# A decoder step on one core: its opening with zero products first, another order of loads, other banks, and squares summed on TensorE

## The chip, the cores and the metric

The kernel runs on one core of one Trainium2 chip. The core has five engines, each with its own instruction stream in a fixed order: TensorE (PE in the profile, its weight loads PEld), VectorE (DVE), ScalarE (ACT), GpSimd (POOL) and SyncE (SP), which here issues all loads and stores. They work on SBUF; TensorE writes into PSUM, eight banks of 128 x 512 fp32, which DVE and ACT read. The metric is device microseconds (us) of one execution. The time before is the median of three runs.

## What is computed

One layer of a hybrid decoder for 512 prompt tokens and 8 x 8 sample tokens, 576 columns in all, of width 1024. The part that the change touches is the first norm and the first columns of the big input product:

```python
def rmsnorm(x, g):
    xf = x.astype(jnp.float32)
    y = xf * lax.rsqrt(jnp.mean(xf * xf, -1, keepdims=True) + EPS)
    return (y * g.astype(jnp.float32)).astype(x.dtype)
...
    h = rmsnorm(x, lp['norm1_g'])
    z = h @ lp['w_in']
...
    qk, mconv_new = causal_dwconv(mconv, z[..., M_QK:M_V], lp['m_conv_w'], lp['m_conv_b'])
...
    li = (z[..., M_I:M_F] + lp['m_i_bias']).astype(f32)
    lf = jax.nn.log_sigmoid((z[..., M_F:M_END] + lp['m_f_bias']).astype(f32))
...
    zr = z[..., R_START:R_END]
    prev = jnp.concatenate([rshift[:, None].astype(zr.dtype), zr[:, :-1]], axis=1)
    xm = zr + (prev - zr) * lp['r_mix']
```

After it come the mLSTM heads, the RWKV-7 recurrence, two gated branches, w_out, a second norm with a convolutional feed-forward part, a third norm with a gate, and the final norm.

## The kernel before

Activations lie with channels on the partitions: x is eight tiles of 128 channels (k = 0 to 7) by 576 tokens, and nearly all work is done in two halves of 288 tokens (`HF`, `half(hf)`). A tile j of `w_in` has 128 output columns; its weights come as two pieces of 128 x 512, one for k 0 to 3 and one for k 4 to 7.

Every wide product is done in three fp32r products: a value is split into a high part (a rounding copy on ACT) and a low part (value less high part, on DVE), and high x high, high x low and low x high are added in one PSUM bank (`half_k`, L190 to L193). So a tile half takes 3 x 8 = 24 products of 128 x 288. `wsplit` (L154, L155) and `wload` (L169, L170) split weights; in the opening the high parts are nh and the low parts nl. `raw_split` (L417, L418) multiplies x by the norm's gain and splits it into xrh and xrl.

The opening (L376 to L463) starts before the norm is known. Three tiles, `lead` = 12, 13, 0, are multiplied with x times gain only, and the norm's factor is applied when they are copied out (`evac_pad` with rs, L355, reading `rsr` in SBUF; without rs it is an ACT copy, L352). The other tiles use `xs1`, the normed and split x (`norm_half`, L268 to L270), as do the 128 columns with the gate rows ("if", L458: the 8 real columns padded to 64, high parts in 64 and low parts in 64, two products for each k).

The norm's factor of a half comes from `add_squares` (ACT squares, L253; for the opening POOL multiplies and adds into acc, L247 and L254), then `rms_half`: three products of acc with a column of ones give the sums by token (L234), DVE scales (L235), POOL takes the power -0.5 (L216), ACT widens to 128 x 384 (L238) and three transposes on TensorE spread it over the partitions (L241). The result is copied to rsr.

PSUM banks have tags: three "d", two "r", one each of "s", "c" and "m". A bank is used again only when its readers are done. Before, tile 12 has two of "d", tile 13 "s" and "c", tile 0 both "r". The gate rows then take the third "d" and an "r", tile 4 two of "d", and tile 8, which comes later by `dense` (L174), "d" banks again.

SP issues the loads in the order in which they are written, apart from waits for buffers: x0 w00 x1 x2 w01 x3 to x7 (first halves; w00 is piece 0 of the first lead tile), cst (identity, ones and masks), w10 w11, the second halves of x, vec, w20 w21. Raw weight pieces have six buffers.

The order of each engine's instructions is set by a planner when the program is built: it runs the program against its own estimate of times, and gives each engine, among the instructions that are ready, the one written first. On the chip that order is fixed. At the very start four products of zeros run on TensorE from a tile `warm` (L394), which DVE clears and into which ACT copies one column; that copy is ACT's first instruction and makes it load its function table.

Of the kernel before, what the change touches and what calls it, by code (L numbers as in the profile page):

```python
# [15 lines left out]
P = 128  # L16
# [79 lines left out]
def build(tc, nc, I, O):  # L96
# [12 lines left out]
    with st0:  # L109
# [119 lines left out]
        def rms_half(pl, acc, hf, pt="m"):  # L229

            pm = bank(pt)
            cols = pl.tile([P, 3], F32, tag="rsc", name="rsc", bufs=2)
            for w, o in enumerate(HB):
                TE.matmul(pm[:, w:w + 1], acc[:, hf * HF + o:hf * HF + o + P], ones[:, 0:1], start=True, stop=True)  # L234
# [4 lines left out]
            b = bank(pt)  # L239
# [136 lines left out]
        with ExitStack() as stn:  # L376
# [14 lines left out]
            S.copy(warm[:, 0:1], nhalf)  # L391
# [4 lines left out]
            xdma(0, 0)  # L396
            wdma(0, 0)
            xdma(1, 0)
            xdma(2, 0)
            wdma(0, 1)  # L400
            for k in range(3, KD):
                xdma(k, 0)
            SY.dma_start(cst, I["cst"])
            wdma(1, 0)
            wdma(1, 1)
# [3 lines left out]
            wdma(2, 0)  # L409
            wdma(2, 1)  # L410
# [3 lines left out]
            lws = [wsplit(raw[0], KD, npool, ("nh", "nl"), 6)]  # L414
            def raw_split(k, hf):
# [5 lines left out]
            xr = []  # L421
            for k in range(KD):
                xr.append(raw_split(k, 0))
                add_squares(npool, acc, xt[k], k, 0, G)
            S.copy(rsr[:, half(0)], rms_half(npool, acc, 0, "m"))
            lws.append(wsplit(raw[1], KD, npool, ("nh", "nl"), 6))
            for k in range(KD):
                add_squares(npool, acc, xt[k], k, 1, G)
            S.copy(rsr[:, half(1)], rms_half(npool, acc, 1, "m"))
            lws.append(wsplit(raw[2], KD, npool, ("nh", "nl"), 6))  # L430
            for k in range(KD):
                for i, j in enumerate(lead):
                    half_k(lps[j][0], lws[i], xr[k], k, KD, slice(0, HF))
            for k in range(KD):
                xr.append(raw_split(k, 1))
            norm_half(npool, xt, rsr[:, half(0)], 0, "norm1_g", xs1)
            for i, j in enumerate(lead):
                for k in range(KD):
                    half_k(lps[j][1], lws[i], xr[KD + k], k, KD, slice(0, HF))

# [7 lines left out]
            w4 = wload(I["w_in"][4], KD)  # L448
            lps["if"] = [bank("d", "pd")]
            lps[4] = [bank("d", "pd")]  # L450
            lps["if"].append(bank("r", "pd"))
            lps[4].append(bank("d", "pd"))
            for hf in range(2):
                if hf:
                    norm_half(npool, xt, rsr[:, half(1)], 1, "norm1_g", xs1)
# [1064 lines left out]
```

## Time and profile before

| what | value |
|---|---|
| median of 3 runs | 1078.46 us (1074.89 to 1079.7) |
| the profiled execution | 1070.66 us |
| its span | 1068.8 us |
| mean granted TensorE clock | 0.996 |
| TensorE busy | 1045.1 us, 98% |
| DVE, ACT, POOL busy | 73%, 48%, 24% |
| moved by DMA | 114.74 MB, mean 107 GB/s |

The profile is of one execution; the time beside the span is what lies around it. A row of the time line has the start, the time, the engine, the line of the code, the operation, output <- inputs, and in brackets how long the engine had stood idle and what released it. A row by groups has the count (x8), the busy time and mean ns behind the bar, and then the idle time in front of the group. fp32 products appear as two records each.

### The profile page before, as it was taken

To read this page: it belongs to the slowest core of one execution; us is meant where nothing else is said; L and a number is where in the kernel's file an instruction comes from. 1 tells how busy PE (TensorE), PEld (TensorE's weight loads), DVE (VectorE), ACT (ScalarE), POOL (GpSimd) and SP (SyncE) were. 2 spreads that over 40 slices of the span, in tenths; PEclk is the share of its full clock that TensorE was granted. 3 is DMA by queue.
4 is the path that set the end of the run, shared out by engine and by line. 5 is a ranking of instruction groups with operands and counts; after the bars stand their busy time and mean duration, and the time that the engine had idled before them with its cause. 6 is when DMAs were issued, how large, how long until landed. Compare 5 with 4: busy or idle time off the path is not lost.

```text
span 1068.8 us, 23108 instructions
## 1 busy us (share of the span) xinstructions
PE 1045.1 (98%) x8991; PEld 1009.0 (94%) x8991; DVE 777.0 (73%) x1645; ACT 508.8 (48%) x1072; POOL 254.5 (24%) x394
## 2 busy tenths in 40 slices
PE   8899999999999999999999999999999999999996
PEld 7899999999989988999999999999999999999996
DVE  7887657876786676356775799945998569975864
ACT  7684634462553344334343465522565236553822
POOL 7622112221131021001401253200343005410300
PEclk9999999999999999999999999999999999999999
DMA  7243412442342322446850312322233322342513
GB/s 252 95 127 93 108 53 58 103 141 60 88 143 75 81 84 91 143 151 234 263 181 1 116 37 93 110 90 75 85 99 97 102 70 90 94 117 67 165 40 123
DMA packets 90894, 114.74 MB, mean 107 GB/s; under 512 B 35617, under 2 KB 45217, under 8 KB 90785
## 3 DMA queue, kind: packets, MB, share of 16 engines
q1 hardware_dynamic: 90784, 113.27, 34.7%
q8 instruction: 70, 1.15, 0.4%
q14 instruction: 40, 0.32, 0.1%
HBM read 94.79 MB, written 18.45 MB: 106 GB/s over the span
## 4 chain that ended last, share of the span: by engine, by line
PE 90%; DVE 4%; DMA 4%; ACT 1%; issue 1%; SPq 0%; POOLq 0%; DVEq 0%; ACTq 0%
PE pd L193 55%; PE pd L306 20%; PE pm L655 1%; PE pm L1106 1%; PE pm L1136 1%; PE pm L835 1%; PE pm L809 1%; DMA yin<-d_y 1%; PE pm L910 1%; DVE xnf L268 1%; PE pm L917 1%; PE pm L1199 1%; PE pm L775 0%; DMA d_y<-og 0%; DMA wr<-i_w_out 0%
## 5 line engine op out<-in xcount | busy, mean ns | idle before, releaser
L169 ACT CAST wh<-wr 128x512 fp32r<-128x512 f32 (+2 forms) x170 | 101.7, 599 | 173.4 <-PE pd L193 140.7
L170 DVE TENSOR_TENSOR wl<-wr,wh 128x512 fp32r<-128x512 f32 (+2 forms) x170 | 118.8, 702 | 82.4 <-ACT wh L169 80.8
L193 PE MATMUL pd<-actl,wh 128*128 128x288 f32 x384 | 111.9, 295 | 0.0
L193 PE MATMUL pd<-acth,wl 128*128 128x288 f32 x384 | 111.4, 295 | 0.0
L193 PE MATMUL pd<-acth,wh 128*128 128x288 f32 x384 | 110.3, 295 | 0.0
L193 PEld LDWEIGHTS pd<-actl,wh 128*128 128x128 f32 x384 | 71.8, 188 | 0.0
L193 PEld LDWEIGHTS pd<-acth,wl 128*128 128x128 f32 x384 | 71.6, 188 | 0.0
L193 PEld LDWEIGHTS pd<-acth,wh 128*128 128x128 f32 x384 | 71.1, 188 | 0.1
L294 ACT CAST wh<-ws 128x512 fp32r<-128x512 f32 x76 | 47.1, 619 | 48.9 <-PE pd L306 24.8
L295 DVE TENSOR_TENSOR wl<-ws,wh 128x512 fp32r<-128x512 f32 x76 | 58.1, 765 | 8.4 <-ACT wh L294 7.9
L300 POOL TENSOR_TENSOR ws<-wr 128x512 f32<-128x512 f32 x19 | 31.7, 1670 | 96.9 <-DVE wl L295 54.1
L294 ACT CAST wh<-wr 128x512 fp32r<-128x512 f32 x57 | 35.3, 619 | 38.5 <-PE pd L306 24.0
L1333 POOL COPY o_f<-u 128x2 f32<-128x2 f32 x22 | 26.6, 1209 | 110.8 <-DVE u L1330 109.2
L295 DVE TENSOR_TENSOR wl<-wr,wh 128x512 fp32r<-128x512 f32 x57 | 39.5, 693 | 7.3 <-ACT wh L294 7.2
L216 POOL TENSOR_TENSOR rsc<-rsc,nhalf 128x3 f32<-128x3 f32 x8 | 9.3, 1167 | 131.1 <-DVE rsc L235 131.1
L1342 DVE SCALAR_TENSOR_TENSOR y<-u,vec,y 128x592 f32<-128x592 f32 x44 | 38.5, 875 | 1.2 <-ACT y L1340 1.0
L253 ACT ACTIVATE sq<-res 128x288 f32<-128x288 f32 x40 | 17.7, 445 | 36.0 <-DVE res L1279 18.5
L193 PE MATMUL pd<-mgh,ol 128*128 128x288 f32 x112 | 33.0, 296 | 0.0
L193 PE MATMUL pd<-mgl,oh 128*128 128x288 f32 x112 | 33.0, 295 | 0.0
L193 PE MATMUL pd<-mgh,oh 128*128 128x288 f32 x112 | 32.8, 295 | 0.0
L1370 DVE TENSOR_TENSOR res<-res,pd 128x288 f32<-128x288 f32 x48 | 20.9, 450 | 15.7 <-PE pd L193 15.5
L193 PE MATMUL pd<-xa0h,wh 128*128 128x288 f32 x86 | 26.4, 307 | 3.0 <-ACT zr L352 1.6
(825 smaller groups left out, 3949.4 us busy)
## 6 DMA issues: line engine op xcount, KB each, us to landing
wr<-i_w_in SPq DMA_DIRECT2D x92, 256.0 KB
wr<-i_f_up SPq DMA_DIRECT2D x88, 256.0 KB
wr<-i_f_down SPq DMA_DIRECT2D x32, 256.0 KB
d_th<-gst SPq DMA_DIRECT2D x16, 288.0 KB
th<-d_th SPq DMA_DIRECT2D x16, 288.0 KB
wr<-i_w_br SPq DMA_DIRECT2D x16, 256.0 KB
wr<-i_w_out SPq DMA_DIRECT2D x16, 256.0 KB
wr<-i_ple_gate SPq DMA_DIRECT2D x16, 256.0 KB
```

The source lines that it names most:

```text
L169: S.copy(wh[:, 0:nk, :], wr[:, 0:nk, :])
L170: V.tensor_tensor(wl[:, 0:nk, :], wr[:, 0:nk, :], wh[:, 0:nk, :], ALU.subtract)
L193: TE.matmul(pm[:, 0:HF], w[:, k % 4, :], a[:, c], start=k == 0 and i == 0, stop=k == n - 1 and i == 2)
L253: S.activation(sq, x[:, c], AF.Square)
L268: V.scalar_tensor_tensor(xn, xt[k][:, c], vcol(gname, k), rs, ALU.mult, ALU.mult)
L294: S.copy(wh, w)
L295: V.tensor_tensor(wl, w, wh, ALU.subtract)
L300: e.tensor_tensor(t, a, b, ALU.add)
L306: TE.matmul(pm[:, 0:HF], w[a][:, k, :], xs[k][b], start=not more and k == 0 and i == 0, stop=k == 3 and i == 2, skip_group_check=more)
L1333: G.tensor_copy(o_f[:, j, 0:2], u[:, TP:TP + 2])
L1342: V.scalar_tensor_tensor(y, u[:, i:i + 592], w(i), y, ALU.mult, ALU.add)
L1370: V.tensor_tensor(x1[m][:, c], x1[m][:, c], pss[hf][:, 0:HF], ALU.add)
```

## The change

It works in the opening alone.

- ACT's first copy goes to a tile of its own (warm1), so the zero products need only DVE's clearing. POOL sets a column of ones (one), which does not come from cst.
- The loads: x0 w00 x1 x2 x3 w01 x4 x5 w10 x6 x7 w11 w20 w21, then cst, the second halves of x, vec.
- All of half 0's `raw_split` stands first, then the splits of the second and third lead tile.
- Half 0's squares: ACT squares all eight x tiles (sq0, four buffers), and TensorE multiplies each with the ones, three products for each k, added up over k in three columns (288 to 290) of one bank "m". POOL adds nothing for half 0. The spread of half 0 is transposed into the same bank, and the norm of half 0 reads it there; the copy to rsr comes behind it.
- Half 1 keeps squares on ACT and additions on POOL; its three sums go into a bank "d", written behind the second lead tile's half 1, its spread into "m".
- Tile 8's products join tile 4's in the opening, in both "r" banks; the gate rows go to "s" and "c".

```diff
-        def rms_half(pl, acc, hf, pt="m"):
-
-            pm = bank(pt)
+        def rms_half(pl, acc, hf, pt="m", sums=None):
+
+            b = sums if acc is None else bank(pt)
+            pm = (sums if sums is not None else b)[:, HF:HF + 3]
             cols = pl.tile([P, 3], F32, tag="rsc", name="rsc", bufs=2)
-            for w, o in enumerate(HB):
-                TE.matmul(pm[:, w:w + 1], acc[:, hf * HF + o:hf * HF + o + P], ones[:, 0:1], start=True, stop=True)
+            if acc is not None:
+                for w, o in enumerate(HB):
+                    TE.matmul(pm[:, w:w + 1], acc[:, hf * HF + o:hf * HF + o + P], ones[:, 0:1], start=True, stop=True)
             V.tensor_scalar(cols, pm[:, 0:3], 1.0 / D, EPS, ALU.mult, ALU.add)
...
-            b = bank(pt)
...
-            S.copy(warm[:, 0:1], nhalf)
+            S.copy(npool.tile([P, 1], F32, name="warm1"), nhalf)
+            one = npool.tile([P, 1], F32, name="one")
+            G.memset(one, 1.0)
...
-            xdma(0, 0)
-            wdma(0, 0)
-            xdma(1, 0)
-            xdma(2, 0)
-            wdma(0, 1)
-            for k in range(3, KD):
-                xdma(k, 0)
+            for what in "x0 w00 x1 x2 x3 w01 x4 x5 w10 x6 x7 w11 w20 w21".split():
...
             SY.dma_start(cst, I["cst"])
-            wdma(1, 0)
-            wdma(1, 1)
             for k in range(KD):
                 xdma(k, 1)
             SY.dma_start(vec[:, KD:NV], I["vec"][:, KD:NV])
-            wdma(2, 0)
-            wdma(2, 1)
...
-            xr = []
+            xr = [raw_split(k, 0) for k in range(KD)]
+            lws.append(wsplit(raw[1], KD, npool, ("nh", "nl"), 6))
+            lws.append(wsplit(raw[2], KD, npool, ("nh", "nl"), 6))
+
+            sums = bank("m")
+            sqs = []
             for k in range(KD):
-                xr.append(raw_split(k, 0))
-                add_squares(npool, acc, xt[k], k, 0, G)
-            S.copy(rsr[:, half(0)], rms_half(npool, acc, 0, "m"))
-            lws.append(wsplit(raw[1], KD, npool, ("nh", "nl"), 6))
+                sqs.append(npool.tile([P, HF], F32, tag="sq0", name="sq0", bufs=4))
+                S.activation(sqs[k], xt[k][:, half(0)], AF.Square)
+                for i, j in enumerate(lead):
+                    half_k(lps[j][0], lws[i], xr[k], k, KD, slice(0, HF))
+                for w, o in enumerate(HB):
+                    TE.matmul(sums[:, HF + w:HF + w + 1], sqs[k][:, o:o + P], one, start=k == 0 and w == 0, stop=k == KD - 1, skip_group_check=True)
+            rs0 = rms_half(npool, None, 0, sums=sums)
+            for k in range(KD):
+                xr.append(raw_split(k, 1))
+            norm_half(npool, xt, rs0, 0, "norm1_g", xs1)
+            S.copy(rsr[:, half(0)], rs0)
             for k in range(KD):
                 add_squares(npool, acc, xt[k], k, 1, G)
-            S.copy(rsr[:, half(1)], rms_half(npool, acc, 1, "m"))
-            lws.append(wsplit(raw[2], KD, npool, ("nh", "nl"), 6))
-            for k in range(KD):
-                for i, j in enumerate(lead):
-                    half_k(lps[j][0], lws[i], xr[k], k, KD, slice(0, HF))
-            for k in range(KD):
-                xr.append(raw_split(k, 1))
-            norm_half(npool, xt, rsr[:, half(0)], 0, "norm1_g", xs1)
             for i, j in enumerate(lead):
                 for k in range(KD):
                     half_k(lps[j][1], lws[i], xr[KD + k], k, KD, slice(0, HF))
+                if i == 1:
+                    rs1 = rms_half(npool, acc, 1, "m", bank("d"))
...
-            w4 = wload(I["w_in"][4], KD)
-            lps["if"] = [bank("d", "pd")]
-            lps[4] = [bank("d", "pd")]
-            lps["if"].append(bank("r", "pd"))
-            lps[4].append(bank("d", "pd"))
+            more = [4, 8]
+            wm = [wload(I["w_in"][j], KD) for j in more]
+            lps["if"] = [bank("s", "pd"), bank("c", "pd")]
+            lps[4] = [bank("d", "pd") for _ in range(2)]
+            lps[8] = [bank("r", "pd") for _ in range(2)]
             for hf in range(2):
                 if hf:
-                    norm_half(npool, xt, rsr[:, half(1)], 1, "norm1_g", xs1)
+                    norm_half(npool, xt, rs1, 1, "norm1_g", xs1)
+                    S.copy(rsr[:, half(1)], rs1)
...
                     if hf:
-                        dense_half(lps[4][hf], w4, xs1, hf, (k,))
+                        for j, w in zip(more, wm):
+                            dense_half(lps[j][hf], w, xs1, hf, (k,))
                 if not hf:
-                    dense_half(lps[4][hf], w4, xs1, hf)
+                    for j, w in zip(more, wm):
+                        dense_half(lps[j][hf], w, xs1, hf)
```

More of the change, by code (lines that the diff above doesn't have):

```diff
@@ L395, in build @@
             SY.dma_start(vec[:, 0:KD], I["vec"][:, 0:KD])
-            xdma(0, 0)
-            wdma(0, 0)
-            xdma(1, 0)
-            xdma(2, 0)
-            wdma(0, 1)
-            for k in range(3, KD):
-                xdma(k, 0)
+            for what in "x0 w00 x1 x2 x3 w01 x4 x5 w10 x6 x7 w11 w20 w21".split():
+                if what[0] == "x":
+                    xdma(int(what[1]), 0)
+                else:
+                    wdma(int(what[1]), int(what[2]))
             SY.dma_start(cst, I["cst"])
-            wdma(1, 0)
-            wdma(1, 1)
             for k in range(KD):
```

## The prediction

> **What bounds the kernel now.** I read the page first: the busy shares, then the chain that ended last.
>
> ```profile
> PE 1045.1 (98%) x8991; PEld 1009.0 (94%) x8991; DVE 777.0 (73%) x1645; ACT 508.8 (48%) x1072; POOL 254.5 (24%) x394
> PE 90%; DVE 4%; DMA 4%; ACT 1%; issue 1%; SPq 0%; POOLq 0%; DVEq 0%; ACTq 0%
> ```
>
> TensorE is the bound: 98% busy, 90% of the chain. An edit of the opening can win only where TensorE stands, runs at a low clock or starts late there. So next came the busy times by stretch (columns: stretch, its length, busy us and count of PE, PEld, DVE, ACT, POOL, then granted clock, DMA share, GB/s), and the inner stretches for PE alone.
>
> ```profile
> 6.00:15.50 9.50, 8.34 (x32) 6.72 (x31) 8.22 (x12) 8.87 (x23) 7.76 (x9) 0.83 1.01 334
> 15.50:32.40 16.90, 16.90 (x130) 16.90 (x130) 15.07 (x33) 10.51 (x25) 11.04 (x10) 0.99 0.67 219
> 32.40:54.10 21.70, 18.50 (x133) 17.58 (x132) 16.25 (x41) 14.05 (x34) 14.93 (x32) 1.00 0.24 79
> 54.10:100.00 45.90, 45.90 (x352) 44.54 (x350) 35.97 (x75) 31.84 (x69) 12.43 (x29) 1.00 0.36 109
> ```
>
> ```profile
> 32.40:38.40 6.00, 6.00 (x45) 1.00 0.00 0
> 38.40:41.00 2.60, 0.96 (x5) 1.00 0.00 0
> ...
> 49.20:51.00 1.80, 0.24 (x2) 1.00 0.77 146
> ```
>
> Four things are to be seen. (1) The first stretch begins at 6 us because no product of the kernel starts before 6.04 (PE's order, below). (2) In 6 to 15.5 us only about 30 products start; at the full rate, 6.00/45 = 0.133 us each by the row 32.40:38.40, they would take 4.0 of the 9.5 us. (3) From 15.5 to 32.4 PE is full. (4) In 32.4 to 54.1 it stands for 21.70 - 18.50 = 3.2 us, nearly all in two holes; from 54.1 to 100 it is full again, so time won before 54 is handed on there.
>
> What fills and empties these stretches is in the groups of 6 to 15.5 us (us in all and mean ns behind the bar), and in PE's order of time (start, us):
>
> ```profile
> L254 POOL TENSOR_TENSOR acc<-acc,sq 128x288 f32<-128x288 f32 x8 | 7.7, 971 | 3.4 <-ACT sq L253 3.2
> L418 DVE SCALAR_TENSOR_TENSOR xrl<-x,vec,xrh 128x288 fp32r<-128x288 f32 x8 | 6.5, 840 | 0.5 <-ACT xrh L417 0.4
> ```
>
> ```profile
> 2.82 3.78 PE L394 MATMUL pm<-warm 128*128 128x256 f32 x8 [2.82 <-ACT warm L391]
> 6.04 0.80 PE L193 MATMUL pd<-xrh,nh 128*128 128x288 f32 x1
> ...
> 40.78 0.37 PE L193 MATMUL pd<-xa0h,wh 128*128 128x288 f32 x1 [1.42 <-DVE k L978]
> 50.84 0.40 PE L193 MATMUL pd<-xa0h,wh 128*128 128x288 f32 x1 [1.56 <-ACT zr L352]
> ```
>
> In stretch (2) the products wait for DVE's low parts (xrl), 840 ns each while POOL adds squares beside them; the DMA share is 1.01, so the loads are the second limit. The two holes of (4) are waits for a PSUM bank of tag "d": one until the gate rows' half 0 is read (L978), one until tile 4 is copied out (L352).
>
> **Part 1, the zero products.** They wait for ACT's write into warm (2.82). Without it they start behind DVE's memset, at about 1.25, and end 1.6 earlier, at about 4.4. The first real product needs nh:
>
> ```profile
> 4.70 0.62 ACT L154 CAST nh<-wr 128x512 fp32r<-128x512 f32 x1 [0.54 <-DMA wr<-i_w_in]
> 7.59 0.62 ACT L154 CAST nh<-wr 128x512 fp32r<-128x512 f32 x1 [0.43 <-DMA wr<-i_w_in]
> ```
>
> so it comes at 5.3 instead of 6.04. I count this at nothing: what follows is bound by arrivals until about 10.5 us, and that hides it. If arrivals were faster it would be worth at most 0.7.
>
> **Part 2, loads in another order.** By their shapes an x half (128x288 f32) has 0.147 MB, a weight piece (128x512) 0.262, cst (128x1000) 0.512. By the second cast above, w01 (fifth large load, 0.97 MB in all) was there at 7.59. The rates by stretch:
>
> ```profile
> 0.00:2.50 2.50, 0.00 (x0) 0.00 (x0) 0.27 (x1) 1.21 (x1) 1.90 (x12) 1.00 0.10 15
> 2.50:5.00 2.50, 2.18 (x5) 1.82 (x6) 0.52 (x1) 1.10 (x4) 1.00 (x7) 1.00 0.90 262
> 5.00:7.50 2.50, 2.50 (x9) 2.14 (x9) 1.70 (x3) 1.97 (x5) 1.07 (x2) 1.00 0.93 284
> 7.50:10.00 2.50, 2.28 (x10) 1.63 (x8) 1.68 (x3) 2.41 (x6) 1.48 (x2) 1.00 1.02 343
> 10.00:12.50 2.50, 1.55 (x8) 1.00 (x7) 2.50 (x4) 2.50 (x7) 2.27 (x4) 0.97 0.98 348
> 12.50:15.00 2.50, 2.50 (x9) 2.17 (x10) 2.50 (x3) 2.49 (x7) 2.44 (x4) 0.50 1.09 349
> ```
>
> They sum to 0.97 MB moved at about 6.0 us, so a load is usable some 1.6 us after its bytes. In the new order w10 is behind 1.67 MB, w11 behind 2.23, w21 behind 2.75: usable at about 9.9, 11.5 and 13.0 (estimates from these rates). Before, w10 stood behind the 0.512 MB of cst, and its cast came at 11.93. cst is needed only for the spread at 20 us or later. The second halves of x now stand behind 3.26 MB instead of 2.74, about 1.5 us later, and are needed by products at 20; w20 and w21 pass them on SP's queue.
>
> **Part 3, order on ACT, DVE and POOL.** What each step takes, by line (min/median/max ns):
>
> ```profile
> L417 ACT ACTIVATE xrh<-x,vec x16: 519/522/536, 3.6 to 26.6; 128x288 fp32r<-128x288 f32 x16
> L418 DVE SCALAR_TENSOR_TENSOR xrl<-x,vec,xrh x16: 503/740/1061, 4.2 to 27.9; 128x288 fp32r<-128x288 f32 x16
> L155 DVE TENSOR_TENSOR nl<-wr,nh x6: 677/692/1290, 5.3 to 21.4; 128x512 fp32r<-128x512 f32 x6
> L253 ACT ACTIVATE sq<-x x14: 426/428/445, 5.7 to 19.9; 128x288 f32<-128x288 f32 x14
> ```
>
> For half 0 POOL's eight steps go (0.97 us each by the group of L254), so DVE should come near its shortest, 0.51 for an xrl and 0.69 for an nl: 8 x 0.51 + 6 x 0.69 = 8.2 us, inside 4.2 to 14.3. ACT has one square more (0.43). Its 8 xrh, 6 casts and 8 squares are 8 x 0.52 + 6 x 0.62 + 8 x 0.43 = 11.3 us from 3.6, so the squares, last in priority, are done at about 15. PE then has 18 products behind it at 10.5 (tile 12, k 0 to 5) and a supply that keeps it full from there. The squares have four buffers, so ACT's fifth waits for PE's first sum, and half 1's xrh and squares queue behind it: nothing while the early sums run early. POOL's additions for half 1 (8 x 0.97 from about 15.5) end at 23.3, ahead of half 1's sums at about 26.
>
> **Part 4, sums on TensorE.** 24 products with ones replace 3, at fp32 and 128x1. What three cost shows in half 1 of before:
>
> ```profile
> 28.72 0.72 PE L234 MATMUL pm<-cst,acc 128*128 128x1 f32 x6
> 29.30 0.38 PE L193 MATMUL pd<-xrh,nl 128*128 128x288 f32 x1
> ```
>
> 0.58 us for three, so 8 x 0.58 = 4.6 us for the half. In ACT's early idle gaps (before nh at 4.70, x2, w01) three or four squares fit; their sums fall into PE's gaps and are free. I charge four, 2.3 us; the bounds are 0 and 4.6.
>
> Lead stage, new: from 10.5 us 144 - 18 = 126 products x 0.133 = 16.8, plus 2.3, plus 0.58 for half 1's sums, plus one spread of about 0.24, ends at 30.4 against 32.4. The clock takes some of it back: it fell to 0.50 in 12.5 to 15 after a stretch in which PE was busy for 1.55 of 2.50 us. Its waits there were short (us in total, times, longest):
>
> ```profile
> PE pd L193 <- DVE xrl L418: 1.2, 4, 0.3
> ```
>
> The new PE is as patchy in 7 to 10. A second such fall costs up to 1.6 us, none 0; I take 0.7 because the early sums fill half of the gaps. So -1.3 for the stage, bounds -4.3 and +1.9.
>
> [...]
>
> **Part 5, banks.** The gate rows go to "s" and "c", tile 8 to "r"; tile 4 keeps "d". Neither hole of 32.4 to 54.1 has its cause left: -3.2 us, bound 0. Tile 8's products, 48 on both sides, only change place. What is late next is the copy-out of tiles 13 and 0, on which "s" and "r" now depend. Half 0 needs the norm's copy (ACT) and two DVE evictions:
>
> ```profile
> 21.00 3.12 POOL L216 TENSOR_TENSOR rsc<-rsc,nhalf 128x3 f32<-128x3 f32 x1 [1.82 <-DVE rsc L235]
> 24.15 0.51 ACT L238 COPY rsb<-rsc 128x384 f32<-128x384 f32 x1 [3.34 <-POOL rsc L216]
> 25.20 0.49 PE L241 MATMUL pm<-cst,rsb 128*128 128x128 f32 x3
> 25.44 0.38 PE L193 MATMUL pd<-xrh,nh 128*128 128x288 f32 x1
> 27.51 0.39 ACT L425 COPY rsz<-pm 128x288 f32<-128x288 f32 x1
> 28.93 1.79 DVE L268 SCALAR_TENSOR_TENSOR xnf<-x,vec,rsz 128x288 f32<-128x288 f32 x4
> 31.02 0.81 DVE L355 TENSOR_TENSOR zr<-pd,rsz 128x288 f32<-128x288 f32 x2
> 35.00 0.43 ACT L269 CAST xa7h<-xnf 128x288 fp32r<-128x288 f32 x1
> ```
>
> Last sum at about 20.0; then 3.12 + 0.51 + 0.24 = 3.9 to the spread; the norm of half 0 runs 6.1 us (28.93 to 35.00); copy and evictions, if behind it, 0.39 + 0.81 = 1.2: 31.2, that is 0.8 after 30.4. Slipped into gaps, as in before at 31.02, they cost 0. I take 0.5. Reading the spread from PSUM costs nothing by the same line's later rows:
>
> ```profile
> L268 DVE SCALAR_TENSOR_TENSOR xnf<-x,vec,rsz x16: 498/506/674, 28.9 to 42.6; 128x288 f32<-128x288 f32 x16
> L268 DVE SCALAR_TENSOR_TENSOR xnf<-res,vec,pm x16: 500/503/515, 994.4 to 1011.7; 128x288 f32<-128x288 f32 x16
> ```
>
> The one bank "m" now carries the sums and half 0's spread until the norm has read it, so half 1's spread enters at about 31; its norm is wanted at 30.4 + 64 x 0.133 = 38.9. Hidden.
>
> **Sum.** -1.3 - 3.2 + 0.5 = -4.0 us. On the profiled execution (1070.66, of which 1068.8 is span) that is 1066.7. Its 1070.66 lies 7.8 under the median of the runs shown, 1078.46 (1074.89 to 1079.7); I put the difference on the median: 1074.5. Half a per cent, about what a measurement of this kernel can tell from no change, is 5.4 us.
>
> **Rivals.** (A) All sums hide and the clock stays up: 2.3 + 0.7 + 0.5 more, -7.5, 1071.0. For it: ACT idles before each early arrival. Against: the squares are last in priority. (B) The loads do not let the supply come sooner (DMA share 0.9 to 1.09, the same bytes): the lead stage gains nothing, only the holes go, -3.2, 1075.3; the order of loads would not do what it says. (C) The planner orders everything behind the opening anew, and the gain is lost again in later waits: 1078.5. Against: 45.90 of 45.90 busy after 54. (D) Slower: the sums stand late in PE's fixed order, and "s" turns into a wait. The gate rows' half 0 is the first instruction behind the lead products, and everything on PE queues behind it. With the last sum at time t the bank is free at t + 3.9 + 6.1 + 1.2, so PE stands for t - 19.2. The gain of 4.5 is eaten from t = 23.7; with the sums behind half 1's products, t = 30.4, PE stands for 11.2, +6.7, 1085.2. Against: the sums of a k stand ahead of half 1 in the program.
>
> **How the numbers follow.** Forecast 0.40, A 0.26, B 0.17, C 0.09, D 0.08. The forecast's own range is -6.5 to -1.5. The range 1068.0 to 1081.5 takes in A with its bound, B, C, the start of D and some 2 us of scatter of a median; it leaves out the rest of D and a gain of over 10. Faster by over 0.5%: most of A and a third of the forecast, 0.37. Slower by over 0.5%: the worse half of D and scatter, 0.06. Within: 0.57.
>
> **What would show it.** Right: nl of tile 13 ends near 10.5 to 11; PE without holes from there to 50; the last sum near 20; the gate rows start near 30 to 31; no wait for L978 or L352 at about 40 and 50. Wrong: a wait of PE for L355 or the copy to rsz ahead of the gate rows (D), a clock of 0.50 past 13 us (sums dear), a start of tile 13 past 12 us (B), new holes after 54 us (C).

## The result, and the profile after

| | median | range | against before |
|---|---|---|---|
| before (20 executions beside it) | 1074.51 us | 1071.15 to 1079.70 | |
| after (20 executions) | 1081.05 us | 1076.46 to 1084.26 | 1.0056 (95%: 1.0040 to 1.0071) |

The change makes the kernel slower by 0.56%, 6.5 us between the medians. The forecast was 4 us faster. The profiled execution took 1078.1 us, with a span of 1076.2. Two executions that lie far off all others, one of the kernel before with 1130.62 us and one of the kernel with one column and the old banks with 3327.29 us, are in no ratio of this document.

First the busy times by stretch of the kernel after, in the columns that the prediction explained (the stretch, its length, busy us and count of PE, PEld, DVE, ACT, POOL, granted clock, DMA share, GB/s).

```profile
0.00:6.00 6.00, 3.96 (x9) 2.71 (x10) 0.99 (x3) 3.19 (x6) 2.26 (x17) 1.00 0.55 142
6.00:15.50 9.50, 9.50 (x54) 9.50 (x55) 7.13 (x13) 8.11 (x20) 0.27 (x1) 0.64 0.97 331
15.50:32.40 16.90, 16.90 (x121) 16.90 (x120) 11.17 (x24) 9.55 (x24) 8.14 (x9) 0.90 0.70 227
32.40:54.10 21.70, 21.70 (x168) 21.70 (x167) 18.00 (x40) 12.54 (x29) 12.54 (x25) 1.00 0.10 28
54.10:100.00 45.90, 42.32 (x300) 40.99 (x299) 33.99 (x75) 33.88 (x77) 10.57 (x34) 0.96 0.42 124
```

Two rows are as forecast, two are not. TensorE has no gap any more from 6 to 54 us: the supply came sooner, and both holes of 32.4 to 54.1 are gone. But its clock in 6 to 15.5 is 0.64, where it was 0.83 with the engine waiting for data. And from 54.1 to 100, where it was busy for 45.90 of 45.90 us, it now stands for 3.6 us. What it waits for there, and the clock's place, are in the waits of PE from 30 to 100 us (us in all, times, longest) and in PE's order of time of the opening (start, us, line, operation):

```profile
PE pm L609 <- ACT sq L604: 1.8, 1, 1.8
PE pd L193 <- ACT zr L353: 1.2, 1, 1.2
PE pm L910 <- DMA lg<-i_lora_g: 0.4, 1, 0.4
```

```profile
8.18 0.87 PE L431 MATMUL pm<-one,sq 128*128 128x1 f32 x6
8.91 0.59 PE L193 MATMUL pd<-xrl,nh 128*128 128x288 f32 x1
9.30 0.44 PE L193 MATMUL pd<-xrh,nl 128*128 128x288 f32 x1
9.54 0.44 PE L193 MATMUL pd<-xrh,nh 128*128 128x288 f32 x1
9.78 1.27 PE L431 MATMUL pm<-one,sq 128*128 128x1 f32 x6
...
24.89 0.72 PE L431 MATMUL pm<-one,sq 128*128 128x1 f32 x6
...
36.11 0.29 PE L193 MATMUL pd<-xa0h,wh 128*128 128x288 f32 x1
```

Read the distance from one start to the next: 0.133 us at the full rate (prediction), 0.24 us from 9.30 on (9.30, 9.54, 9.78). Three one-column sums, 0.72 us long at full rate (24.89), take 1.27. TensorE runs at half speed there (granted clock 0.50 from 9 to 18 us), and the profile lists no wait of PE from 5.82 to 32 us. The first product of normed data starts at 36.11; before it was 32.45. Later there is a second place: between 100 and 440 us PE waits for tiles that return from a scratch buffer in memory, 4.4 us in all (before: 1.5 for these).

```profile
PE pm L782 <- DMA TT<-scr1t: 3.5, 2, 2.3
PE pm L782 <- DMA TT<-scr0t: 0.9, 2, 0.6
```

### The profile page after: what moved, and what is told of

Its sections match the earlier page's. It is cut to its first block, busy times and chain, and to the rows that moved or that the text cites. A ratio compares the mean times of both kernels' runs of the same rounds, so it can differ in the third digit from the quotient of the medians.

```text
span 1076.2 us, 23180 instructions
## 1 busy us (share of the span) xinstructions
PE 1053.0 (98%) x9033; PEld 1017.3 (95%) x9033; DVE 779.3 (72%) x1645; ACT 509.7 (47%) x1073; POOL 246.1 (23%) x387
## 5 line engine op out<-in xcount | busy, mean ns | idle before, releaser
L170 DVE TENSOR_TENSOR wl<-wr,wh 128x512 fp32r<-128x512 f32 (+2 forms) x170 | 115.5, 683 | 77.7 <-ACT wh L169 75.1
L295 ACT CAST wh<-wr 128x512 fp32r<-128x512 f32 x57 | 35.3, 619 | 37.5 <-PE pd L307 23.3
L1377 DVE TENSOR_TENSOR res<-res,pd 128x288 f32<-128x288 f32 x48 | 20.9, 452 | 15.6 <-PE pd L193 15.5
L255 DVE TENSOR_TENSOR acc<-acc,sq 128x288 f32<-128x288 f32 x42 | 19.0, 457 | 12.9 <-ACT sq L254 12.3
```

What stands on the lines that cost most here:

```text
L170: V.tensor_tensor(wl[:, 0:nk, :], wr[:, 0:nk, :], wh[:, 0:nk, :], ALU.subtract)
L255: (eng or V).tensor_tensor(acc[:, c], acc[:, c], sq, ALU.add)
L295: S.copy(wh, w)
L1377: V.tensor_tensor(x1[m][:, c], x1[m][:, c], pss[hf][:, 0:HF], ALU.add)
```

## The experiments

Two theories came out of the two traces. CLOCK: the one-column sums let TensorE's clock fall. LATER: something behind the opening, which the bank part touches, is now the limit, and gains made before it are lost. Rivals: the sums cost only their own work; the banks are harmless. All ratios are to the kernel before, timed beside it.

| kernel | zero products, loads | splits first, spread read in PSUM | half 0's sums | banks | ratio (95%) |
|---|---|---|---|---|---|
| before | old | old | POOL | old | 1 |
| zero and loads | new | old | POOL | old | 0.9981 (0.9965 to 0.9997) |
| POOL sums, old banks | new | new | POOL | old | 0.9943 (0.9922 to 0.9964) |
| 64 columns, old banks | new | new | TensorE, 64 columns | old | **0.9911 (0.9890 to 0.9931)** |
| 16 columns, old banks | new | new | TensorE, 16 columns | old | 0.9951 (0.9932 to 0.9970) |
| 1 column, old banks | new | new | TensorE, 1 column | old | 0.9968 (0.9951 to 0.9985) |
| after | new | new | TensorE, 1 column | new | 1.0056 (1.0040 to 1.0071) |
| 64 columns | new | new | TensorE, 64 columns | new | 1.0015 (0.9989 to 1.0040) |
| POOL sums | new | new | POOL | new | 1.0008 (0.9984 to 1.0032) |
| banks only | old | old | POOL | new | 1.0043 (1.0026 to 1.0059) |
| 1 column only | old | old | TensorE, 1 column | old | 1.0088 (1.0063 to 1.0112) |

### POOL sums, ones 64 columns wide, banks only, zero products and loads

The first four went together. The second multiplies the squares with 64 columns of ones in place of one, so that each instruction keeps its place and only its width differs:

```diff
-            one = npool.tile([P, 1], F32, name="one")
+            one = npool.tile([P, 64], F32, name="one")
...
-                    TE.matmul(sums[:, HF + w:HF + w + 1], sqs[k][:, o:o + P], one, ...
+                    TE.matmul(sums[:, HF + 64 * w:HF + 64 * w + 64], sqs[k][:, o:o + P], one, ...
```

The others undo the sums alone (`add_squares` on POOL again), or put one part alone into the kernel before: the banks, or the zero products and the order of loads.

> The changed kernel with half 0's squares added up on POOL again and three sums with ones from cst, as before; zero products first, the order of loads, the order of the splits and the banks stay changed. CLOCK and WORK both: the lead stage loses the sums; first normed product at 30 to 32 us instead of 36.1 (32.4 in before). If the whole loss comes from the sums, the ratio to before is 0.995 to 0.998. Rival LATER (the wide lookahead, tile 8 and its banks, costs as much behind 50 us as it saves in the two holes, because the engines behind TensorE get their input from the same chain of weight buffers and loads): the ratio is 1.000 to 1.003 although the lead stage is as short as or shorter than in before.

> The changed kernel with one edit: the ones that the squares are multiplied with are 64 columns wide instead of 1 (each sum is written 64 times, every 64th column is read). TensorE's order stays the same but for these widths. Theory CLOCK (the 128x1 products move so little that the granted clock falls to half at about 8.3 us and stays there to 18.6 although TensorE is full, which costs the lead stage about 4 to 5 us): with 64 columns the granted clock in 6 to 15.5 us is 0.83 or more instead of 0.64, the first product with a normed x starts at 31 to 33 us instead of 36.1, and the time falls by 3 to 5 us against the changed kernel (ratio to before 1.001 to 1.003). Rival WORK (the sums cost only the time they take, and the clock falls because the supply of products is patchy, as it did in before at 12.4 us): the clock stays near 0.64, the first normed product stays at 36 +- 0.7 us, the ratio stays at 1.005 to 1.006.

> The kernel before with the last part of the change alone: gate rows in s and c, tile 8 beside tile 4 in both r banks in the opening. Forecast (the two holes at 39.1 to 40.8 and 49.1 to 50.8 go and the end comes 3.2 us earlier): ratio 0.997. Rival LATER (no gain at the end, because the loads of the shift state and the copies behind the weight buffers start no earlier, and TensorE stands later instead): the holes go, the load of the shift state is issued at 48 us or later, TensorE waits between 55 and 90 us for 2 us or more, ratio 0.999 to 1.003.

> The kernel before with the zero products first and the new order of loads alone (sums, order of splits and banks as before). Forecast: the first products of the second lead tile come at 10.5 to 12 us instead of 13.7, the first normed product at 30.5 to 31.5 instead of 32.4, ratio 0.998 to 0.999. Rival BYTES (all loads share one rate, so what comes earlier for one comes later for another): 32 to 33 us, ratio 0.9995 to 1.002.

Measured: 1.0008, 1.0015, 1.0043, 0.9981. PE's order of time and the stretch of 6 to 15.5 us of the kernel with 64 columns:

```profile
8.06 0.78 PE L431 MATMUL pm<-one,sq 128*128 128x64 f32 x6
8.65 0.38 PE L193 MATMUL pd<-xrl,nh 128*128 128x288 f32 x1
8.87 0.29 PE L193 MATMUL pd<-xrh,nl 128*128 128x288 f32 x1
8.99 0.30 PE L193 MATMUL pd<-xrh,nh 128*128 128x288 f32 x1
9.13 0.78 PE L431 MATMUL pm<-one,sq 128*128 128x64 f32 x6
```

```profile
6.00:15.50 9.50, 9.50 (x80) 9.50 (x79) 7.01 (x13) 8.03 (x20) 0.19 (x1) 1.00 1.02 345
```

The same instructions in the same order, each sum 64 times as wide: the clock stays at 1.00, 80 products start where 54 did, and the first normed product comes at 32.26 in place of 36.11. The last sum starts at 20.03, where the prediction had it, in place of 24.89. So in this order the clock falls with sums of one column (0.64) and not with sums of 64 (1.00), as CLOCK had it. But the kernel that has the lead back is still no faster than before: LATER holds too. The banks alone, without any sums on TensorE, show it too. The stretches of that kernel and its waits of PE, 30 to 100 us:

```profile
32.40:54.10 21.70, 21.70 (x165) 21.56 (x165) 16.37 (x41) 14.02 (x34) 14.58 (x32) 1.00 0.26 87
54.10:100.00 45.90, 43.70 (x318) 42.29 (x317) 35.19 (x75) 32.09 (x71) 9.97 (x30) 0.96 0.35 106
```

```profile
PE pm L604 <- ACT sq L599: 1.8, 1, 1.8
PE pd L193 <- ACT zr L352: 0.3, 1, 0.3
```

The 3.2 us of holes before 54 are gone and 2.2 us of waits stand behind 54, with a clock of 0.96 after them. The kernel is slower by 0.43%, and these rows make up the smaller part of that: at its squares (ACT's `sq` of line 599, 76.50) it is only 0.85 us behind the kernel before, and most of the loss comes later, where PE's waits of 100 to 1080 us sum to 15.6 us against 9.7.

The zero products and loads alone bring the first normed product to 32.15, only 0.3 us sooner than in the kernel before, as the rival BYTES had it, although the ratio is in the range of the forecast. The granted clock of that profile is 0.50 from 10 to 12.5 us, with no sums there.

### The old banks in the new opening, and the one-column sums alone

The bank part was undone in three of the kernels (the new lines are those of before):

```diff
-            more = [4, 8]
-            wm = [wload(I["w_in"][j], KD) for j in more]
-            lps["if"] = [bank("s", "pd"), bank("c", "pd")]
-            lps[4] = [bank("d", "pd") for _ in range(2)]
-            lps[8] = [bank("r", "pd") for _ in range(2)]
+            w4 = wload(I["w_in"][4], KD)
+            lps["if"] = [bank("d", "pd")]
+            lps[4] = [bank("d", "pd")]
+            lps["if"].append(bank("r", "pd"))
+            lps[4].append(bank("d", "pd"))
```

> The changed kernel with two parts undone: half 0's squares are added on POOL as before, and the gate rows, tile 4 and tile 8 have their old banks; zero products first, the loads, the order of the splits and the spread read in PSUM stay. CLOCK (TensorE's clock falls while it works through the one-column sums): no sums in the first 15 us, so the clock stays at 0.95 or more in 6 to 15.5 us and the first normed product starts at 31 to 32. LATER (the banks part costs about 0.4% behind the opening): the same opening with the new banks came to 1.0008, so this gives 0.996 to 0.998, and the loads behind the opening are issued 0.5 to 1.5 us earlier than before, up to the last output. If the banks part is harmless and 1.0008 is what the splits and the spread cost: 1.000 to 1.002.

> The changed kernel with the ones 64 columns wide, and the gate rows, tile 4 and tile 8 in their old banks. CLOCK: 1.00 in 6 to 15.5 us as with the new banks, first normed product at 32 to 32.5. LATER: 1.0015 - 0.0043 = 0.997, range 0.995 to 0.999; the two waits for a bank of 32 to 54 us are back (together some 3 us) and it is still no slower. If the holes were real losses: 1.003 to 1.005.

> The changed kernel with its one-column sums, and the gate rows, tile 4 and tile 8 in their old banks. CLOCK: 0.6 to 0.7 in 6 to 15.5 us and the first normed product at 35.5 to 36.5, as in the changed kernel. If cold clock and banks add up: 1.0056 - 0.0043 = 1.0013, range 0.999 to 1.003, the loads behind the opening 3 to 5 us late against before at 48 to 52 us. If the sums alone are the loss (banks harmless): 1.005 to 1.006. If the holes were real losses: above 1.007.

> The kernel before with one part of the change alone: half 0's squares are added up by 24 one-column products with ones on TensorE, in place of POOL's additions; zero products, loads and banks as before. CLOCK: granted clock 0.5 to 0.7 over most of 8 to 18 us though the engine is counted as busy, first normed product 3 to 5 us late (35.5 to 37.5 against 32.45), ratio 1.002 to 1.005. WORK (the sums cost only their own time at full clock, 24 x 0.2 us less the gaps that they fill): clock as before (0.83 in 6 to 15.5 us), first normed product 0 to 2.5 us late, ratio 0.999 to 1.002.

Measured: 0.9943, 0.9911, 0.9968 and 1.0088. All four lie further out than expected. The banks cost 0.65%, 1.04% and 0.88% in the three pairs (with POOL sums, 64 columns, one column), one and a half to two and a half times the 0.43% of the old opening, and the holes do not come back with the old banks. All that PE waits for in 30 to 100 us in the kernel with POOL sums and old banks is one row:

```profile
PE pd L458 <- DVE xa4l L271: 0.8, 2, 0.6
```

So the holes belonged to the old order of the opening; the new order fills them without new banks. Two things of these profiles were not expected. The kernel with POOL sums and old banks has a granted clock of 0.64 with no sum of squares on TensorE in this stretch:

```profile
6.00:15.50 9.50, 7.68 (x32) 6.30 (x31) 9.13 (x12) 8.45 (x21) 7.37 (x8) 0.64 0.99 342
```

PE waits there for xrl, 1.0 us at the longest. So the clock fell beside a patchy supply too (7.68 of 9.50 us busy), as the prediction had feared, and to leave the sums off TensorE was no safeguard. And the profiles with 64 columns and with one column, old banks, have their first normed products at 37.97 and 38.18: both began at half speed (last section), and only their distances from that product can be compared.

Where the banks' loss begins is read across three engines, in the time line of after (first fence), of the kernel with POOL sums and old banks (second) and of the kernel before (third):

```profile
47.13 0.94 DVE L356 TENSOR_TENSOR zr<-pd,rsz 128x224 f32<-128x224 f32 x4
...
47.94 0.30 PE L193 MATMUL pd<-xa7h,wl 128*128 128x288 f32 x1
48.08 0.30 PE L463 MATMUL pd<-xa0h,wif 128*128 128x288 f32 x1
...
53.63 0.48 ACT L982 ACTIVATE q<-pd,vec 4x288 f32<-4x288 f32 x1
...
81.52 0.77 ACT L604 ACTIVATE sq<-xk,vec 128x576 f32<-128x576 f32 x1
```

```profile
32.05 0.29 PE L458 MATMUL pd<-xa0h,wif 128*128 128x288 f32 x1
...
34.64 0.81 DVE L356 TENSOR_TENSOR zr<-pd,rsz 128x288 f32<-128x288 f32 x2
...
38.56 0.30 PE L458 MATMUL pd<-xa0h,wif 128*128 128x288 f32 x1
...
44.82 0.48 ACT L975 ACTIVATE q<-pd,vec 4x288 f32<-4x288 f32 x1
...
71.49 0.77 ACT L597 ACTIVATE sq<-xk,vec 128x576 f32<-128x576 f32 x1
```

```profile
32.45 0.30 PE L458 MATMUL pd<-xa0h,wif 128*128 128x288 f32 x1
...
38.77 0.93 DVE L355 TENSOR_TENSOR zr<-pd,rsz 128x224 f32<-128x224 f32 x4
...
75.65 0.77 ACT L597 ACTIVATE sq<-xk,vec 128x576 f32<-128x576 f32 x1
```

Half 1's gate rows need a free bank. In the new banks it is "c", which tile 13's half 1 holds until DVE has copied it out, behind the norm of half 1: 48.07 us (47.13 + 0.94). They start at 48.08, behind 48 products of tiles 4 and 8. With the old banks it is the "r" that tile 0's half 0 leaves at 35.45 (34.64 + 0.81), and they start at 38.56. ScalarE reads them (q) 17.5 us after the first normed product in the one (53.63 - 36.11) and 12.8 us after in the other (44.82 - 32.05). What is queued behind q in ScalarE's fixed order moves along, down to the squares on which PE then waits 1.8 us: they come 45.4 us after the first normed product (81.52 - 36.11) against 39.4 (71.49 - 32.05). In the kernel before, with its holes, it was 43.2 (75.65 - 32.45).

The same two distances, to the squares and to the end of the span, part the loss of the banks into what is near and what comes later (us from the first normed product, one profiled execution each, old banks, then new):

| opening | to the squares | to the end |
|---|---|---|
| POOL sums | 39.4, 45.5 | 1032.0, 1038.0 |
| 64 columns | 38.7, 44.6 | 1030.0, 1038.7 |
| 1 column | 38.7, 45.4 | 1030.9, 1040.1 |
| that of before | 43.2, 44.0 | 1036.3, 1045.0 |

In the new opening about 6 us of the loss are there at the squares, and 0 to 3 come behind them. In the old opening 0.8 of 8.7 us are there at the squares, and the rest comes later. (The profiled execution of before is one of its fastest; between the medians that loss is 4 us.)

The one-column sums in the old opening lost more than CLOCK gave: the first normed product came at 41.16, in place of 35.5 to 37.5. The stretches show a fall (the last two with PE alone):

```profile
6.00:15.50 9.50, 7.53 (x53) 7.42 (x52) 6.44 (x12) 8.00 (x20) 1.60 (x2) 0.87 0.96 325
15.50:32.40 16.90, 15.03 (x85) 14.68 (x85) 11.95 (x24) 9.67 (x23) 6.13 (x8) 0.67 0.69 225
10.00:12.50 2.50, 1.20 (x11) 1.00 1.02 365
12.50:15.00 2.50, 1.84 (x8) 0.59 1.03 335
```

In the second stretch 85 products start where 130 did, at a clock of 0.67. But this run does not show CLOCK. Up to 11.2 us, with 13 of the 24 sums among the products, the clock is 1.00; then PE waits 2.0 us for nh, and the clock falls behind that wait. Whether the sums or the wait brought the fall, and what part of the lost 8.7 us (41.16 - 32.45) is waiting for the late sums, was not taken apart.

### Which piece of the banks part, and how wide the ones must be

To the kernel with 64 columns and old banks, the new banks of the gate rows alone, with tile 8 left out of the opening:

```diff
-            lps["if"] = [bank("d", "pd")]
-            lps[4] = [bank("d", "pd")]
-            lps["if"].append(bank("r", "pd"))
-            lps[4].append(bank("d", "pd"))
+            lps["if"] = [bank("s", "pd"), bank("c", "pd")]
+            lps[4] = [bank("d", "pd") for _ in range(2)]
```

To the kernel with 64 columns and all new banks, other buffers for tile 8's split weights:

```diff
-            wm = [wload(I["w_in"][j], KD) for j in more]
+            wm = [wload(I["w_in"][4], KD), wload(I["w_in"][8], KD, npool, ("nh", "nl"), 6)]
```

The third is the kernel with old banks and ones 16 columns wide.

> The changed kernel with ones 64 columns wide and only half of the banks part: the gate rows in s and c, tile 4 in d, but tile 8 not in the opening (it comes later by dense, as before). The banks part cost 0.9 to 1.0% in two pairs of kernels; this run and the next ask which piece of it. BUFFERS (tile 8 in the opening holds the two free pairs of split-weight buffers wh and wl until half 1's products, so ScalarE's next weight cast waits, and all that is queued behind it): the loss needs tile 8, so this stays at 0.989 to 0.993, ScalarE's waits for wh on TensorE in 28 to 100 us sum to under 6 us, and the two waits for a bank are gone. BANKS (the gate rows behind the copy-out of tile 13 are the loss): 0.998 to 1.002.

> The changed kernel with ones 64 columns wide and its new banks, tile 8 in the opening, but tile 8's split weights lie in the lead tiles' buffers nh and nl, which tile 12 leaves free, and not in wh and wl. BUFFERS: ScalarE's waits for wh on TensorE in 28 to 100 us fall from 10.7 us (changed kernel) to under 6, ScalarE's first mix of a gate input (48.06 us with wh held) starts before 45, and the ratio falls from 1.0015 to 0.991 to 0.996. If the loss is that tile 8's 48 products are used up early and leave nothing to fill TensorE's waits of 60 to 82 us: still 1.000 to 1.003, with the wait of some 1.8 us for the squares at 75 to 82 us.

> The changed kernel with ones 16 columns wide and the old banks: between one column (0.9968) and 64 columns (0.9911), each instruction in the same place. CLOCK, by the width of the products: 16 columns keep TensorE little busier than one, the opening runs at half clock in most executions, 0.995 to 0.998 and a mean recorded clock of 0.993 or less where the opening's fall is recorded. If any width above one is enough: 0.990 to 0.992. The work itself differs by under 1 us among the three.

Measured: 1.0000 (0.9980 to 1.0021), 1.0006 (0.9988 to 1.0024), 0.9951 (0.9932 to 0.9970). BUFFERS falls: without tile 8 in the opening nearly the whole loss is there, 0.9911 to 1.0000. Two of its signs failed too: ScalarE still waits 7.1 us for wh in 28 to 100 us, and one of the two waits of PE for a bank is back, 1.8 us for ACT's copy-out zr at 51.06. The edit with other buffers did not do what it was for. ScalarE's waits, 28 to 100 us, in that kernel:

```profile
ACT wh L169 <- PE pd L193: 9.6, 7, 3.6
...
ACT q L982 <- PE pd L463: 5.5, 1, 5.5
```

It still waits 9.6 us for wh, and 5.5 us more for the gate rows of half 1; that run tells nothing for or against. Of the gate banks there are two, and the last two kernels leave one of each:

```diff
-            lps["if"] = [bank("s", "pd"), bank("c", "pd")]
+            lps["if"] = [bank("s", "pd"), bank("r", "pd")]
```

and, for the mirror image,

```diff
-            lps["if"] = [bank("s", "pd"), bank("c", "pd")]
+            lps["if"] = [bank("d", "pd"), bank("c", "pd")]
```

> As the kernel with the gate rows in s and c (ratio 1.000), but half 1's gate rows in r, which tile 0's half 0 leaves, in place of c, which is free only when tile 13's half 1 has been copied out (VectorE ends that at 44.13 us there, behind the whole norm of half 1). HALF 1 IN c IS THE LOSS: half 1's gate products stand between tile 4's again and end before 44 us, ScalarE no longer waits 2.5 us for them, ratio 0.989 to 0.994. HALF 0 IN s IS THE LOSS (tile 4's half 0 goes ahead of the gate rows): still 0.998 to 1.002. BOTH: 0.994 to 0.998.

> The mirror image: half 0's gate rows in d, as before, half 1's in c. HALF 1 IN c IS THE LOSS: 0.998 to 1.002, half 1's gate products start after 44 us, and ScalarE waits for them. HALF 0 IN s IS THE LOSS: 0.989 to 0.994. BOTH: 0.994 to 0.998.

Measured: 0.9953 (0.9934 to 0.9972) and 0.9962 (0.9937 to 0.9986). Each half of the loss is there alone: 0.0042 for half 0 in s, 0.0051 for half 1 in c, beside 0.0089 for both together. The intervals only just clear that of the old banks (0.9890 to 0.9931), and each size is known to about 0.003, so it is not shown that the two are alike or that they add up. A part can be chance: by span times clock, an estimate (last section), six of the twelve executions with half 0 in s and three of the nine with half 1 in c began at half speed, and one of the six with the old banks. With half 1 in c ScalarE stands for them (waits, 28 to 100 us):

```profile
ACT q L978 <- PE pd L461: 2.5, 1, 2.5
```

and the distance from first normed product to squares is 43.1 us; with half 0 in s it is 40.0, but the first normed product itself is 1.5 us later (33.01 against 31.56), behind a wait of 1.5 us for the spread.

### The copy-out ahead of the norm

The change had also moved the copy of the norm's factor, which tile 13's copy-out reads, behind the norm. If that is why s and c are late, moving it back must take the loss away with the banks left as they are:

```diff
+                    S.copy(rsr[:, half(1)], rs1)
                     norm_half(npool, xt, rs1, 1, "norm1_g", xs1)
-                    S.copy(rsr[:, half(1)], rs1)
```

Half 1's copy alone and both copies (gate banks only), both copies with all new banks, both copies with the old banks as the control; all with 64 columns:

> The kernel with 64 columns and the gate rows in s and c (tile 8 not in the opening; 1.000), with one line moved: the copy of half 1's norm factor to rsr stands ahead of half 1's norm, as before the change, and not behind it. COPY-OUT (c is dear because tile 13's half 1 is copied out only behind the whole norm): VectorE ends that copy-out near 39 to 40 us in place of 44.13, half 1's gate products stand among tile 4's, ratio 0.993 to 0.997, that is the loss of half 1 in c (0.0051) gone. If the loss is the bank c itself, or the order that the planner makes of it whatever the copy: 0.998 to 1.002.

> The same with both copies to rsr ahead of their norms. COPY-OUT: tile 13's half 0 is out some 5 us sooner too, the gate rows of half 0 stand ahead of tile 4's again; 0.990 to 0.995, since three evictions of 0.4 us each now stand ahead of half 0's norm. Otherwise: no better than with half 1's copy alone, or 0.998 to 1.002.

> The changed kernel with 64 columns, all its new banks with tile 8 in the opening (1.0015), and both copies to rsr ahead of their norms. COPY-OUT: 0.991 to 0.997. If tile 8 in the opening has a price of its own that the other kernels hid: 0.997 to 1.001.

> The control: 64 columns, old banks (0.9911), both copies to rsr ahead of their norms. COPY-OUT: nothing that stands in its way waits for tile 13, so no gain; 0.990 to 0.995, with half 0's norm later by up to 1.3 us. If moving the copies is a gain in itself, whatever the banks: under 0.989.

Measured: 0.9986 (0.9967 to 1.0005), 0.9996 (0.9976 to 1.0016), 0.9969 (0.9951 to 0.9987) and, for the control, 1.0112 (1.0085 to 1.0140). COPY-OUT falls as the one cause. The moved copy does what it should nearby: with half 1's copy first, q comes 14.5 us after the first normed product, where it was 17.2. But of the 0.9% it brings back 0.0 to 0.5%, and in the control it costs 2.0%. Where the control loses is far behind, in its stretches and its waits of PE, 200 to 440 us:

```profile
205.00:225.00 20.00, 17.60 (x175) 14.66 (x174) 8.35 (x20) 5.46 (x13) 0.72 (x3) 0.83 0.58 157
290.00:310.00 20.00, 17.34 (x124) 13.67 (x123) 7.10 (x17) 3.47 (x7) 0.72 (x3) 0.74 0.49 124
```

```profile
PE pm L780 <- DMA TT<-scr1t: 3.7, 2, 2.4
PE pd L193 <- ACT og L1095: 2.8, 1, 2.8
PE pm L780 <- DMA TT<-scr0t: 2.7, 1, 2.7
```

The first and the third are the waits for tiles from the scratch buffer again, and the clock of the stretches around the two longest is 0.83 and 0.74. Without the moved copies these two waits were 1.2 and 0.3 us. From the first normed product to the squares the control is 3.5 us longer than with the copies behind the norm (42.2 against 38.7), to the end of the span 21 us. The planner had put the whole program in another order, and 170 to 390 us behind the edit PE had, by these waits, less work beside the round trips. So a bank or a copy in the opening has two prices: the wait that it makes nearby, and the order that the planner then finds for everything behind. Both are read in the traces; the second was not predicted by any of the theories.

## Why the prediction was wrong

The change is three gains and two losses. Read down the table of ratios, one part at a time: zero products and loads -0.19%, splits first and spread read in PSUM -0.38%, sums on TensorE with 64 columns -0.32%, one column in place of 64 +0.57%, new banks +0.88%: together +0.56%. By the other way through the table, the banks first, they are +1.04% for the banks and +0.41% for the one column. Each difference is known to about 0.3%, and each contains the planner's other order. The forecast time, 1074.5, is the median that the kernel before came to in more executions (1074.51); that 1081.05 lies inside the range, which was counted from a median of three 4 us higher, is luck: slower by over 0.5% was given 0.06.

- **Parts 1 to 3, zero products, loads and supply: right in direction, too large in size.** The zero products end at 5.03, as their own row less 1.57 gives, not at 4.4, and the first real product came at 5.82 (forecast 5.3). The first cast of the second lead tile came at 10.85, where its load was to be usable at 9.9 (11.93 before). Without one-column sums, the first normed product came at 31.5 to 32.3 in the profiles of the two POOL-sum kernels and of 64 columns with new banks, beside a forecast of 30.4 plus 0.7 for clock and 32.45 before.
- **Part 4, the term that failed first: 0.7 us for the clock, 1.6 at most.** I took the one fall that the profile of before showed as the bound, and argued that sums fill gaps and so hold the clock up. With sums of one column the clock fell although the gaps were filled: 3.85 us of the lead stage (36.11 against 32.26), and 0.41% and 0.57% of the whole in the two pairs (1.0056 against 1.0015, 0.9968 against 0.9911). The last sum came at 24.89 and not at 20.0 for the same reason: in the same order with 64 columns it is at 20.03. Beside a patchy supply, the other cause that I named, the clock fell as well (0.64 with POOL sums and old banks, 7.68 of 9.50 us busy). Why a full queue did not keep it up with one column (9.50 of 9.50 us busy, 0.64 granted) no run here shows.
- **Part 5, the bank holes at -3.2: wrong in sign.** "Neither hole of 32.4 to 54.1 has its cause left" was right, and is as true without the new banks, through the new order alone. "From 54.1 to 100 PE is full again, so time won before 54 is handed on there" is the step that failed: the holes went, and 3.6 us of waits and a clock of 0.96 stood behind 54. A full PE showed that it had work to fill with, not that it set the end. When it ran ahead it met ScalarE's and VectorE's chain from half 1's norm and gate rows to the squares.
- **Part 5, the copy-out at 0.5: the step that passed by the loss.** I followed the copy-out of half 0 (s) and not that of half 1 (c), which ends at 48.07, behind all of half 1's norm; in the kernel before it ended at 39.70 (38.77 + 0.93), ahead of the norm's second half, and the diff showed its copy moved behind. The banks were priced at -2.7 in all and cost 8.6 to 10.4 us between the medians of the three pairs, a part by s and a part by c. About 6 us of it are near, there at the squares, and the rest comes later, with the planner's other order. Half 1 in c makes most of the near part: with it alone the squares are 43.1 us after the first normed product, where they are 38.7 with the old banks and 40.0 with half 0 in s. That the late copy-out alone makes it is not shown: to move the copy of half 1 ahead brought the squares only 1.2 us nearer (42.0 after the first normed product, 43.2 without) and the ratio from 1.0000 to 0.9986.
- **Rivals.** C, at 0.09, was nearest: everything behind the opening in a new order, "the gain lost again in later waits". I held 45.90 of 45.90 busy after 54 against it, which is an argument about the old order. The one slower rival, D, put its wait at half 0's gate rows and got its price from late sums; no rival joined the sums to the clock.
- **Not priced at all:** the order of splits, with the spread read in PSUM. It gave 0.38% with the old banks and POOL sums, where the distance from first normed product to squares is 39.4 us and not 43.2.

## What to carry to other kernels

Before work is moved to another bank, follow the last reader of each half of the bank's old content to its own place in its engine's order, and not only of the half that comes first. A stage in which the main engine is full is no proof that time won ahead of it is handed on, and where a planner sets the order, even a small edit in an opening is to be timed in parts: here three gains of 0.2 to 0.4% were hidden by two losses of 0.4 to 0.6% and 0.7 to 1.0%. Sums by a product with ones had better have width: 64 equal columns in place of one won 0.4 to 0.6% here, and with the old banks that kernel takes 1064.82 us, 0.9911 (0.9890 to 0.9931) of before, the best of all that ran.

## What the runs showed of the hardware

**Width and clock.** With old banks and the same order, 1, 16 and 64 columns gave 0.9968, 0.9951 and 0.9911. Each execution has a span and a mean granted clock; their product is taken here as the span at full clock, an estimate. With 64 columns five of six executions have a clock of 0.996 to 0.998 and products of 1059.5 to 1060.4; with 16, one of twelve has such a pair (0.998 and 1058.8), and nine have 0.988 to 0.993 with 1057.6 to 1059.1, that is, by this estimate, the same work in spans of 1066.6 to 1071.5 us in place of 1060.9. With one column none of eleven has such a pair: five have a clock of 0.988 to 0.992, and six have a high clock (0.995 to 0.997) and a product of 1064.4 to 1069.8. The one of these six that was profiled began at half speed (next), and a high clock with a product of over 1064 is read here as a sign of that. Why the clock goes with the width was not shown.

**A clock column that does not see it.** In the profile of one column with old banks the stretch and PE's order read:

```profile
6.00:15.50 9.50, 9.50 (x45) 9.50 (x44) 6.16 (x12) 7.92 (x19) 0.67 (x1) 1.00 1.01 351
```

```profile
17.37 0.44 PE L193 MATMUL pd<-xrh,nl 128*128 128x288 f32 x1
17.61 0.44 PE L193 MATMUL pd<-xrh,nh 128*128 128x288 f32 x1
17.85 0.44 PE L193 MATMUL pd<-xrl,nh 128*128 128x288 f32 x1
```

The column says 1.00, and products start every 0.24 us, half speed, from the first one to 20.98. The slowest execution of the 64-column kernel with old banks (1069.66), which is the one profiled, looks the same up to 20.63, with sums in between up to 16.88. The profile with POOL sums and new banks also begins so, but is at full speed from 13.69 on. So some executions begin at half speed and are not marked, with one column, with 64 and with POOL sums, and 64 columns do not bring the clock up: the three profiles with such sums that begin so reach full speed at 20.0 to 21.2. Where the clock was up it held beside them: 1.00 in the 64-column profile with the new banks (6 to 15.5 us), and 0.996 to 0.998 in the five executions above. Among the executions that by the estimate did not begin so, the five with one column have 0.988 to 0.992 and the five with 64 have 0.996 to 0.998, with medians of 1069.45 and 1064.38 us. The distance between starts is the safer reading: 0.24 us here under a column of 1.00, against 0.133 at full rate. What decides whether an execution begins so stays open.
